# The first adaLN modulation loaded and computed in two halves of 512 features, in a two-layer diffusion trunk

## The chip, the cores and the metric

The kernel runs on one core of a Trainium2 chip. The metric is the device time of one execution in microseconds; the figure given is the median of several executions.

## The reference

The reference is a trunk of two layers over 256 context tokens and 256 latent tokens of width 1024 in float32. Each layer normalises the tokens and modulates them by a conditioning vector (adaLN), projects them by one wide matrix `w_in`, feeds three token mixers (an S5 state-space model, a bidirectional SSD, a windowed attention), merges them, and then runs 16 SwiGLU experts. What the change touches is the modulation at the head of layer 0. Cut to that:

```python
def rmsnorm(x, g):
    xf = x.astype(F32)
    y = xf * lax.rsqrt(jnp.mean(xf * xf, axis=-1, keepdims=True) + EPS)
    return (y * g.astype(F32)).astype(x.dtype)
...
```

The conditioning vectors `c` and `c_ctx` pass through SiLU and are multiplied with `w_mod` (1024 x 6144 for a layer), plus `b_mod`. Of the six vectors of 1024 features that come out, the first two are the shift `sh1` and the scale `sc1` of the first normalisation: the tokens become `rmsnorm(x, norm1_g) * (1 + sc1) + sh1`, with one pair for the context and one for the latent tokens.

## The kernel before, in words

The kernel is written as a sequence of tile operations, and a scheduler orders the instructions of each engine from that sequence. Within an engine the order is then fixed: an instruction that waits holds up all behind it. SP issues the loads, in the order in which the scheduler places them. PSUM banks come from three rings (`mm` 3, `ps` 4, `s5` 1); weight tiles `w` of 0.52 MB come from a ring of three (line 107), with the split into a high and a low part, `wh` on ACT (line 114) and `wl` on DVE or POOL in turn (line 117).

At the head of layer 0, `mixing` (line 464) loads the tokens into `xna` and `xnb` (line 506). `mod_load(k)` (line 490) loads, for a block k of 128 features, the columns of `w_mod` for shift (kind 0) and scale (kind 1): two loads of 0.52 MB each, in runs of 128 floats, 512 B. Blocks 0 to 4 are loaded ahead of the norm, blocks 5 to 7 after the first input projection weights. Blocks 0 and 1 lie in `rb8` tiles, the others in `m8` tiles.

`norm_rows` (line 527) goes over the blocks. For each it calls `mod_unit` (line 148) for both kinds: eight products with `sil` (32 columns of the array each, four column groups, 128 weight columns wide, line 152), a copy of the four partial sums to SBUF on ACT (line 154), a product with `sel2` that sums the groups and turns the result into a column (line 155), and an affine step on ACT that adds the bias and multiplies by the norm weight (line 160). Then `transposed` (line 246) turns the four token tiles of this block (line 249), ACT modulates them into `hrow` (line 252), and DVE splits them into `hh` and `hl` (lines 534 and 535).

The input projection of the S5 part follows in two halves `kh` of four blocks (lines 565 to 577), into four `ps` banks, with three products per weight (`mm3`, lines 126 and 129). Its result goes to DRAM through `us` (lines 561 and 562) and is read back by the S5 loop. That loop also needs the S5 parameters, which `s5_params` computes from 18.7 us on with many small operations on DVE (lines 301 to 309), four copies on ACT (line 421), and a chain on POOL (lines 438 to 443, and 671 to 673). They are independent of the modulation, but are queued on the same engines. `todo` (line 580) holds the other modulations; `mod_group` (line 163) makes them later, between other work. The small projection at line 753 makes the SSD's step sizes.

Of the kernel before, what the change touches and what calls it, by code (L numbers as in the profile page):

```python
# [24 lines left out]
F32 = mybir.dt.float32  # L25
# [3 lines left out]
AF = mybir.ActivationFunctionType  # L29
OP = mybir.AluOpType  # L30
# [41 lines left out]
def tile_trunk(ctx: ExitStack, tc: tile.TileContext, a, out, dbg=None, stop=None):  # L72
# [22 lines left out]
    def K(name):  # L95
        lo, hi = K_OFF[name]
        return kc[:, lo:hi]

    def C(name):
        lo, hi = C_OFF[name]  # L100
        return cl[:, lo:hi]
# [43 lines left out]
    names = ("sh1", "sc1", "g1", "sh2", "sc2", "g2")  # L145
    todo = []

    def mod_unit(l, kind, k, w):
        ps = bank("mm")
        for i in range(8):  # L150
            j = i % 4
            PE.matmul(ps[32 * j:32 * j + 32, :128], sil[:, i, :], w[:, i, :], start=i < 4, stop=i >= 4)
        part = small.tile([128, 128], F32, name="cpart", bufs=2)
        S.activation(part, ps[:, :128], AF.Copy)
        PE.matmul(ps[:, 256:258], part, K("sel2"), start=True, stop=True)
        if k == 0:
            mods[l][names[kind]] = const.tile([128, 8, 2], F32, name="mcol%d_%d" % (l, kind))
        bo = (l * 6 + kind) * 8 + k
        ng = {1: C("norm1"), 4: C("norm2")}.get(kind)
        S.activation(mods[l][names[kind]][:, k, :], ps[:, 256:258], AF.Identity, bias=bmod[:, bo:bo + 1],  # L160
                     scale=1.0 if ng is None else ng[:, l * 8 + k:l * 8 + k + 1])

    def mod_group(l, kind, h):
        ps = bank("mm")
# [303 lines left out]
    def mixing(l, mods):  # L468
# [17 lines left out]
        junk = m8("junk")  # L486
        xv = lambda tt: half(xna[tt // 2], tt)
        if full:
            mw = {}
            slab = Slab(rb, 2)  # L490

            def mod_load(k):
                if k < 2:
                    t = rb.tile([128, 2048], F32, name="rb8", tag="rb8", bufs=NRB)
                else:
                    t = m8("mw").rearrange("p a b -> p (a b)")
                ws = t[:, :1024], t[:, 1024:]
                mw[k] = [w.rearrange("p (i c) -> p i c", i=8) for w in ws]
                for kind in range(2):
                    SP.dma_start(mw[k][kind], a["w_mod"][l][:, kind * D + k * 128:kind * D + k * 128 + 128]  # L500
                                 .rearrange("(i p) c -> p i c", p=128))

            for k in range(0):
                mod_load(k)
            for st, nm in enumerate(("ctx", "x")):
                SP.dma_start(xna[st].rearrange("p (q e) c -> p q (e c)", q=2), a[nm].rearrange("(q p) d -> p q d", p=128))
            for k in range(0, 5):
                mod_load(k)
            xn = norm_tok([0, 1, 2, 3], xv, xv, lambda tt: half(junk, tt))
        else:  # L510
            xo = X["x"]
            xn = {}
            for st in range(2):
                rs = rs_tok(X["xsq"], [2 * st, 2 * st + 1])
                for i in range(2):
                    tt = 2 * st + i
                    xn[tt] = xv(tt)
                    if i:
                        S.activation(xn[tt], xo[:, tt, :], AF.Copy, scale=rs[:, i:i + 1])
                    else:  # L520
                        V.tensor_scalar(xn[tt], xo[:, tt, :], rs[:, i:i + 1], None, op0=OP.mult)
            xsave = dram.tile([256, D], F32, name="xsave")
            SP.dma_start(xsave.rearrange("(q p) d -> p q d", p=128), xo[:, 2:4, :])
            X["stack"].close()
        bst = ExitStack()
        bp = bst.enter_context(tc.tile_pool(name="mixB", bufs=1, side="right", reuse_waits="tile"))
        def norm_rows(ks):
            for k in ks:
                if full:
                    for kind in range(2):  # L530
                        mod_unit(0, kind, k, mw[k][kind])
                h = transposed(xn, [0, 1, 2, 3], k, mods["sc1"], mods["sh1"], bp, "t2", T2,
                               ("mm" if k % 2 else "s5") if full else "ps")
                V.tensor_copy(r(hh[:, k, :]), h)
                (G if k % 2 and not full else V).tensor_tensor(r(hl[:, k, :]), h, hh[:, k, :], op=OP.subtract)
# [28 lines left out]
        if full:  # L564
            ub = [bank() for _ in range(4)]
            for kh in range(2):
                norm_rows(range(4 * kh, 4 * kh + 4))
                wu = []
                for i in range(0, 4, 2):
                    wu.append(load_w(a["w_in"][l], 4 * kh, 4, 128 * i, 256))  # L570
                if kh == 0:
                    for k in range(5, 8):
                        mod_load(k)
                for i in range(0, 4, 2):
                    wh, wl = wu[i // 2]
                    mm3(ub[i:i + 2], wcols(wh, wl), [lambda m, k=k: hv(4 * kh + k, 0, 512) for k in range(4)], kh == 0, kh == 1)
            for m in range(4):
                ev_u(m, ub[m])
        else:
            norm_rows(range(8))  # L580
            win(0, [0] * 4, ev_u)
# [1014 lines left out]
```

## Time and profile before

| | us |
|---|---|
| median of three executions | 2152.39 |
| lowest of three | 2150.96 |
| highest of three | 9962.31 |
| the profiled execution, its own time | 2158.89 |
| its span, first to last instruction | 2157.1 |
| PE (TensorE) busy in the span | 1887.0 |
| DVE (VectorE) busy | 1049.4 |
| ACT (ScalarE) busy | 560.5 |
| POOL (GpSimd) busy | 585.1 |

Busy times are sums over the whole span, over stages with different limits. PEld are TensorE's weight loads, which overlap its products; a float32 product is two instructions in the trace. The granted clock of TensorE was 0.945 of full speed over the span. The profile moved 561.7 MB, 260 GB/s on average.

### The profile page before, as it was taken

Reading aid. Unit: us, or ns where it says so; the run is one execution under the profiler, and the core shown is the slowest. Engines: PE = TensorE matmul, PEld = TensorE weight load, DVE = VectorE, ACT = ScalarE, POOL = GpSimd, SP = SyncE. Lnnn points to the kernel's source line nnn. Section 1 sums busy time; section 2 is a strip of 40 time slices with the busy share of each in tenths; the row PEclk is TensorE's granted clock in tenths of the full one; section 3 lists DMA queues with packets and bytes.
Section 4 is the critical chain, followed back from the end, with each engine's and each line's share of the span. In section 5 each row is a group of like instructions: output and inputs, shape, how many; then the busy total and the mean of one; then the engine's idle time right before and its main releaser. Section 6 shows DMA issues by size and latency. Waiting matters only on the chain.

```text
span 2157.1 us, 29435 instructions
## 1 busy us (share of the span) xinstructions
PE 1887.0 (87%) x11292; PEld 1127.7 (52%) x11292; DVE 1049.4 (49%) x2250; ACT 560.5 (26%) x1216; POOL 585.1 (27%) x644
## 2 busy tenths in 40 slices
PE   6899989999999999787887798989999898777775
PEld 4577767788787333222222576778898432111111
DVE  6888787763246226221212569777856322112112
ACT  4425634442343120000000433534444110000000
POOL 1645476542242000200001425475633100000000
PEclk9899999999999999999999897988999899999998
DMA  9464333336346989799999265342476999999996
GB/s 275 152 189 130 109 90 108 100 104 215 98 147 243 412 324 418 319 420 420 419 420 362 77 200 166 119 125 74 110 248 205 420 420 420 419 420 420 420 420 260
DMA packets 214460, 561.70 MB, mean 260 GB/s; under 512 B 41328, under 2 KB 129840, under 8 KB 165936
## 3 DMA queue, kind: packets, MB, share of 16 engines
q1 hardware_dynamic: 182016, 541.82, 66.8%
q10 hardware_dynamic: 32304, 18.00, 3.0%
q8 instruction: 89, 1.46, 0.3%
q14 instruction: 51, 0.42, 0.1%
HBM read 552.00 MB, written 7.77 MB: 260 GB/s over the span
## 4 chain that ended last, share of the span: by engine, by line
PE 48%; DMA 33%; DVE 11%; POOL 3%; issue 2%; ACT 2%; SPq 1%; DVEq 0%; POOLq 0%; ACTq 0%
PE bk_mm L126 12%; PE bk_mm L129 6%; DMA xw<-w_e_up 6%; DMA xw<-w_e_gate 4%; DMA xw<-w_e_down 4%; DMA xq<-w_e_down 4%; PE bk_mm L1415 4%; DMA rb<-w_e_gate 3%; DMA rb<-w_e_down 3%; DMA xq<-w_e_up 3%; PE bk_ps L1304 3%; DMA w<-w_in 2%; PE bk_mm L1431 2%; PE bk_mm L1445 2%; DMA xq<-w_e_gate 2%
## 5 line engine op out<-in xcount | busy, mean ns | idle before, releaser
L126 PE MATMUL bk_mm<-hh,wh 128*128 128x512 f32 (+1 forms) x704 | 255.0, 375 | 8.3 <-ACT xp L806 4.6
L126 PE MATMUL bk_mm<-hl,wh 128*128 128x512 f32 (+1 forms) x704 | 247.7, 365 | 0.0
L117 POOL TENSOR_TENSOR wl<-w,wh 128x1024 fp32r<-128x1024 f32 x64 | 156.8, 2450 | 221.1 <-ACT wh L114 175.8
L114 ACT ACTIVATE wh<-w 128x1024 fp32r<-128x1024 f32 x140 | 148.1, 1058 | 227.2 <-PE bk_mm L126 107.7
L129 PE MATMUL bk_mm<-hh,wl 128*128 128x512 f32 (+1 forms) x704 | 161.9, 360 | 0.0
L126 PEld LDWEIGHTS bk_mm<-hh,wh 128*128 128x128 f32 x704 | 140.0, 199 | 32.0 <-ACT xp L806 6.0
L126 PEld LDWEIGHTS bk_mm<-hl,wh 128*128 128x128 f32 x704 | 139.8, 199 | 17.4 <-issue 1.0
L117 DVE TENSOR_TENSOR wl<-w,wh 128x1024 fp32r<-128x1024 f32 x76 | 101.6, 1338 | 77.0 <-ACT wh L114 36.3
L129 PEld LDWEIGHTS bk_mm<-hh,wl 128*128 128x128 f32 x704 | 119.1, 195 | 17.6 <-issue 1.2
L1450 DVE SCALAR_TENSOR_TENSOR hd<-fth,bk_mm 64x512 f32<-64x512 f32 x16 | 10.9, 681 | 220.3 <-ACT fth L1448 220.3
L1435 DVE SCALAR_TENSOR_TENSOR YE<-bk_mm,grow 32x512 f32<-32x512 f32 x64 | 43.9, 687 | 133.8 <-PE bk_mm L1431 133.0
L1448 ACT ACTIVATE fth<-bk_mm 64x512 f32<-64x512 f32 x16 | 9.4, 590 | 364.5 <-PE bk_mm L1445 364.5
L1415 PE MATMUL bk_mm<-xw,xeB 128*64 128x512 f32 x368 | 88.0, 601 | 15.6 <-DMA xw<-w_e_up 9.5
L1467 DVE SCALAR_TENSOR_TENSOR YE<-bk_mm,grow 32x512 f32<-32x512 f32 x64 | 44.0, 687 | 104.7 <-PE bk_mm L1462 103.9
L1445 PE MATMUL bk_mm<-xw,xeB 128*32 128x512 f32 x296 | 68.0, 597 | 18.5 <-DMA xw<-w_e_gate 9.8
L609 POOL MEMSET rb<- 128x256 f32 x2 | 1.2, 588 | 286.1 <-DMA rb<-w_e_gate 272.9
L1418 ACT ACTIVATE fth<-bk_mm 128x512 f32<-128x512 f32 x16 | 9.6, 597 | 239.7 <-PE bk_mm L1415 239.7
L169 PE MATMUL bk_mm<-w,sil 128*32 128x128 f32 x1280 | 60.8, 291 | 9.5 <-DMA w<-w_mod 8.5
L1431 PE MATMUL bk_mm<-xw,hT 128*64 128x512 f32 x232 | 62.0, 628 | 7.2 <-ACT hT L1426 5.2
L1392 PE MATMUL bk_ps<-YE,Gt 128*128 128x512 f32 x128 | 61.0, 610 | 6.3 <-DVE YE L1435 3.2
L1415 PEld LDWEIGHTS bk_mm<-xw,xeB 128*64 128x64 f32 x368 | 24.1, 136 | 77.5 <-issue 35.7
L126 PE MATMUL bk_mm<-yh,wh 128*128 128x512 f32 (+1 forms) x192 | 63.9, 349 | 0.8 <-ACT yh L741 0.8
(564 smaller groups left out, 3914.7 us busy)
## 6 DMA issues: line engine op xcount, KB each, us to landing
xw<-w_e_up SPq DMA_DIRECT2D x70, 1024.0 KB, 19.9
xw<-w_e_gate SPq DMA_DIRECT2D x62, 1024.0 KB, 19.9
xw<-w_e_down SPq DMA_DIRECT2D x58, 1024.0 KB, 19.8
w<-w_in SPq DMA_DIRECT2D x92, 512.0 KB, 4.2
w<-w_mod SPq DMA_DIRECT2D x80, 512.0 KB, 3.8
rb<-w_e_down SPq DMA_DIRECT2D x36, 1024.0 KB, 19.9
rb<-w_e_gate SPq DMA_DIRECT2D x35, 1024.0 KB, 14.2
rb<-w_e_up SPq DMA_DIRECT2D x33, 1024.0 KB, 19.9
```

Source lines behind the costliest of these rows:

```text
L114: S.activation(r(hi), raw, AF.Copy)
L117: e.tensor_tensor(r(lo), raw, hi, op=OP.subtract)
L126: PE.matmul(ps, wh(m, k), xv, start=first and k == 0 and i == 0, stop=False)
L129: PE.matmul(ps, wl(m, k), xs[k](m)[0], start=False, stop=last and k == n - 1)
L169: PE.matmul(ps[32 * j:32 * j + 32, :128], sil[:, 2 * u + i, :], w[:, i, pair(j) if kind in (3, 4) else slice(j * 128, j * 128 + 128)], sta ...
L1304: PE.matmul(ps[:, si * w_:si * w_ + w_], x[:, tt, pair(k)], oh[tt][:, e0:e1, :], start=q == 0, stop=q == 1)
L1392: PE.matmul(ps, Gt[:, tt - tts[0], e // ne, :], YE[:, tt // 2 if full else 0, n, :], start=True, stop=True)
L1415: PE.matmul(ps[64 * n:64 * n + 64, :], xeT(k, e), w[:, n * 512:n * 512 + 512], start=k == 0, stop=k == 7)
L1431: PE.matmul(py[64 * n:64 * n + 64, :], hT[:, k // 4, k % 4, :], w, start=k == 0, stop=k == 7)
L1435: V.scalar_tensor_tensor(YE[q0:q0 + 32, si, n, :], py[o:o + 32, :], 0.5, g2[o:o + 32, si, n * 512:n * 512 + 512], op0=OP.mult, op1=OP.mult)
L1445: PE.matmul(pg[o:o + 32, :], xeT(k, e), w[:, n * 512:n * 512 + 512], start=k == 0, stop=k == 7)
L1467: V.scalar_tensor_tensor(YE[q0:q0 + 32, 0, n, :], py[o:o + 32, :], 0.5, g2[o:o + 32, 1, n * 512:n * 512 + 512], op0=OP.mult, op1=OP.mult)
```

## The change

The modulation of the first normalisation is made in two halves h of 512 features. `mod_load(h, u, kind, own)` loads, for a half h and a kind, 512 rows (half u of the contraction) by 512 columns: 1.05 MB in runs of 512 floats, 2 KB. There are eight such loads where there were sixteen; the four of half 0 stand ahead of the norm, the four of half 1 after the first weights of the input projection. `mod_half` uses four column groups of 32 for two kinds times two parities, 512 columns wide, copies the whole bank on ACT, transposes it in four pieces (four products with `ident`), and lets DVE sum the two partial sums (a reduction straight from PSUM), multiply by the norm weight and add the bias. It is called once per half, ahead of `norm_rows`.

```diff
-    def mod_unit(l, kind, k, w):
+    def mod_half(h, ws):
         ps = bank("mm")
...
+        for kind, u, w in ws:
+            for i in range(4):
+                j = 2 * kind + i % 2
+                PE.matmul(ps[32 * j:32 * j + 32, :], sil[:, 4 * u + i, :], w[:, i, :], start=u == 0 and i < 2, stop=u == 1 and i >= 2)
+        part = small.tile([128, 512], F32, name="mpart", bufs=1)
+        S.activation(part, ps, AF.Copy)
+        pt = bank("mm")
+        for j in range(4):
+            PE.transpose(pt[:, j * 128:j * 128 + 128], part[:, j * 128:j * 128 + 128], ident)
+        pv = pt.rearrange("p (j k a s) -> p k j s a", j=4, k=2, a=2)
+        for kind in (1, 0):
+            if h == 0:
+                mods[0][names[kind]] = const.tile([128, 8, 2], F32, name="mcol0_%d" % kind)
+            dst = mods[0][names[kind]][:, 4 * h:4 * h + 4, :]
+            bc = lambda v: v[:, :, None].to_broadcast([128, 4, 2])
+            V.tensor_reduce(dst, pv[:, kind, :, 0:2, :], axis=AX.X, op=OP.add)
+            if kind:
+                V.tensor_tensor(dst, dst, bc(C("norm1")[:, 4 * h:4 * h + 4]), op=OP.mult)
+            bo = kind * 8 + 4 * h
+            V.tensor_tensor(dst, dst, bc(bmod[:, bo:bo + 4]), op=OP.add)
...
+            def mod_load(h, u, kind, own):
+                w = (rb.tile([128, 2048], F32, name="rb8", tag="rb8", bufs=NRB) if own
+                     else m8("mw").rearrange("p a b -> p (a b)")).rearrange("p (i c) -> p i c", i=4)
+                c0 = kind * D + h * 512
+                SP.dma_start(w, a["w_mod"][l][512 * u:512 * u + 512, c0:c0 + 512].rearrange("(i p) c -> p i c", p=128))
+                mw.setdefault(h, []).append((kind, u, w))
...
-            for k in range(0, 5):
-                mod_load(k)
+            for u in range(2):
+                for kind in range(2):
+                    mod_load(0, u, kind, u == 0)
...
             for k in ks:
-                if full:
-                    for kind in range(2):
-                        mod_unit(0, kind, k, mw[k][kind])
...
             for kh in range(2):
+                mod_half(kh, mw[kh])
                 norm_rows(range(4 * kh, 4 * kh + 4))
...
                 if kh == 0:
-                    for k in range(5, 8):
-                        mod_load(k)
+                    for u in range(2):
+                        for kind in range(2):
+                            mod_load(1, u, kind, False)
```

The scheduler orders all engines anew. The first place is DVE shortly after the norm. Line numbers of the changed kernel are those of its own text: its 309, 311, 314, 317 and 339 are lines 301, 303, 306, 309 and 331 before (S5 parameters), its 260 is 252, its 429 is 421, and 534 and 535 are the same; `rb` is the S5 parameters' scratch, `hh` and `hl` the split tokens, `mcol` the modulation columns. Before:

```order
L306 SCALAR_TENSOR_TENSOR rb_112<-rb_112 128x96 x6
L534 CAST hh<-hrow 128x512
L309 TENSOR_TENSOR rb_112<-rb_112 128x96 x2
L535 TENSOR_TENSOR hl<-hrow,hh 128x512
L303 TENSOR_SCALAR rb_112<-rb_112 128x96
L534 CAST hh<-hrow 128x512
L303 TENSOR_SCALAR rb_112<-rb_112 128x96
L535 TENSOR_TENSOR hl<-hrow,hh 128x512
L301 TENSOR_SCALAR rb_112<-rb_112 128x96 x2
L306 SCALAR_TENSOR_TENSOR rb_112<-rb_112 128x96 x2
```

After:

```order
L309 TENSOR_SCALAR rb_112<-rb_112 128x96 x2
L314 SCALAR_TENSOR_TENSOR rb_112<-rb_112 128x96
L165 TENSOR_REDUCE mcol_1_182<-bk_mm 128x8
L165 TENSOR_REDUCE mcol_0_186<-bk_mm 128x8
L314 SCALAR_TENSOR_TENSOR rb_112<-rb_112 128x96
L167 TENSOR_TENSOR mcol_1_182<-mcol_1_182,cl 128x8
L169 TENSOR_TENSOR mcol_0_186<-mcol_0_186,cl 128x8
L309 TENSOR_SCALAR rb_112<-rb_112 128x96
L311 TENSOR_SCALAR rb_112<-rb_112 128x96
L169 TENSOR_TENSOR mcol_1_182<-mcol_1_182,cl 128x8
L314 SCALAR_TENSOR_TENSOR rb_112<-rb_112 128x96
L339 CAST rb_112<-rb_112 128x96
```

Before, the S5 operations there were interleaved with the first splits `hh` and `hl`, one block after the other; now the two reductions and the three further steps of the first half stand there, and the first split comes later, behind more S5 operations.

The second place is DVE in the second half, where `hh` of block 5 was made. Before:

```order
L309 TENSOR_TENSOR rb_113<-rb_112 128x64 x2
L309 TENSOR_TENSOR rb_112<-rb_113 128x64 x4
L534 CAST hh<-hrow 128x512
L309 TENSOR_TENSOR rb_113<-rb_112 128x64 x2
L535 TENSOR_TENSOR hl<-hrow,hh 128x512
L309 TENSOR_TENSOR rb_112<-rb_112 128x64 x2
```

After:

```order
L317 TENSOR_TENSOR rb_112<-rb_113 128x64 x4
L317 TENSOR_TENSOR rb_113<-rb_112 128x64 x2
L165 TENSOR_REDUCE mcol_1_182<-bk_mm 128x8
L165 TENSOR_REDUCE mcol_0_186<-bk_mm 128x8
L317 TENSOR_TENSOR rb_112<-rb_112 128x64 x2
L317 TENSOR_TENSOR rb_112<-rb_112 128x32
L167 TENSOR_TENSOR mcol_1_182<-mcol_1_182,cl 128x8
L169 TENSOR_TENSOR mcol_0_186<-mcol_0_186,cl 128x8
```

The reduction of the second half has come to the place where a split of block 5 stood, behind the same S5 operations.

The third place is ACT, from the last modulations of the second half to the last `hrow`; `sp_aa` and `sp_ab` are the copies of the S5 parameters. Before:

```order
L160 ACTIVATE mcol_1_191<-bk_mm,cl 128x2
L252 ACTIVATE hrow<-bk_mm,mcol_0_177,mcol_1_191 128x256 x2
L154 ACTIVATE cpart<-bk_mm 128x128 x2
L421 ACTIVATE sp_aa<-rb_113 64x8x4x9
L421 ACTIVATE sp_ab<-rb_113 64x8x4x9
L160 ACTIVATE mcol_0_177<-bk_mm,cl 128x2
L154 ACTIVATE cpart<-bk_mm 128x128
L421 ACTIVATE sp_aa<-rb_113 64x8x4x9
L421 ACTIVATE sp_ab<-rb_113 64x8x4x9
L160 ACTIVATE mcol_1_191<-bk_mm,cl 128x2
L252 ACTIVATE hrow<-bk_s_478,mcol_0_177,mcol_1_191 128x256 x2
```

After:

```order
L114 ACTIVATE wh<-w 128x1024 x2
L155 ACTIVATE mpart<-bk_mm 128x512
L429 ACTIVATE sp_aa<-rb_113 64x8x4x9
L429 ACTIVATE sp_ab<-rb_113 64x8x4x9
L429 ACTIVATE sp_aa<-rb_113 64x8x4x9
L429 ACTIVATE sp_ab<-rb_113 64x8x4x9
L260 ACTIVATE hrow<-bk_s_326,mcol_0_186,mcol_1_182 128x256 x2
L260 ACTIVATE hrow<-bk_mm,mcol_0_186,mcol_1_182 128x256 x2
L260 ACTIVATE hrow<-bk_s_346,mcol_0_186,mcol_1_182 128x256 x2
```

Before, two of the four `hrow` pairs of the second half stood ahead of the S5 copies (the earlier one is not in this piece) and two behind them (the later one is not in it); now all four stand behind the four copies, the last one outside the piece.

## Rows read from the trace of the kernel before

**Rows 1.** Windows by stage: length, busy (count) of PE, PEld, DVE, ACT, POOL, clock, DMA, GB/s.

```profile
46.00:54.00 8.00, 7.01 (x105) 5.73 (x96) 7.97 (x48) 3.96 (x10) 0.61 (x1) 1.00 0.51 139
...
100.00:310.00 210.00, 195.82 (x1576) 149.13 (x1572) 173.32 (x316) 102.88 (x254) 113.58 (x128) 0.97 0.45 133
...
400.00:620.00 220.00, 220.00 (x1193) 174.55 (x1182) 100.98 (x180) 80.11 (x143) 85.94 (x76) 1.00 0.43 130
...
880.00:1185.00 305.00, 256.73 (x1053) 77.85 (x1050) 58.34 (x88) 13.50 (x26) 6.36 (x10) 0.99 1.00 412
1185.00:1690.00 505.00, 452.31 (x3414) 377.81 (x3416) 354.43 (x710) 204.56 (x446) 240.22 (x247) 0.89 0.50 157
```

**Rows 2.** Chain of waits, 0 to 33 us: start, length, what.

```profile
11.10 1.69 SPq L500
...
23.71 1.74 SPq L110
...
25.49 7.79 DMA w<-w_in
```

**Rows 3.** Timeline of PE, 13 to 46 us: start, length, what, idle before.

```profile
13.16 1.08 PE L152 MATMUL bk_mm<-rb,sil 128*32 128x128 f32 x16 [13.16 <-DMA rb<-w_mod]
...
24.22 1.08 PE L152 MATMUL bk_mm<-mw,sil 128*32 128x128 f32 x32
25.80 0.64 PE L152 MATMUL bk_mm<-mw,sil 128*32 128x128 f32 x16 [0.50 <-DMA mw<-w_mod]
...
32.91 0.80 PE L126 MATMUL bk_ps<-hh,wh 128*128 128x512 f32 x1 [1.48 <-ACT wh L114]
...
43.79 1.98 PE L129 MATMUL bk_ps<-hh,wl 128*128 128x512 f32 x8
```

**Rows 4.** Timeline of DVE, 18 to 53 us, columns as in rows 3.

```profile
18.69 0.20 DVE L303 TENSOR_SCALAR rb<-rb 128x96 f32<-128x96 f32 x1
...
23.61 0.43 DVE L534 CAST hh<-hrow 128x512 fp32r<-128x512 f32 x1 [1.06 <-ACT hrow L252]
...
34.39 2.00 DVE L117 TENSOR_TENSOR wl<-w,wh 128x1024 fp32r<-128x1024 f32 x1 [1.70 <-ACT wh L114]
...
52.78 0.42 DVE L534 CAST hh<-hrow 128x512 fp32r<-128x512 f32 x1
```

**Rows 5.** Waits of DVE, 18.69 to 62.2 us: for whom, total, times, longest.

```profile
DVE hh L534 <- ACT hrow L252: 2.9, 5, 1.1
```

**Rows 6.** Timeline of POOL, the chain after DVE, columns as in rows 3.

```profile
62.25 0.27 POOL L438 TENSOR_TENSOR rb<-sp_e8r,rb 128x32 f32<-128x32 f32 x1 [4.59 <-DVE rb L309]
...
81.17 0.72 POOL L673 TENSOR_TENSOR rb<-rb 128x256 f32<-128x256 f32 x1
```

**Rows 7.** Windows by DMA load, columns as in rows 1.

```profile
3.00:11.00 8.00, 0.00 (x0) 0.00 (x0) 1.42 (x13) 3.23 (x9) 0.00 (x0) 1.00 1.01 386
...
18.00:22.00 4.00, 4.00 (x42) 2.83 (x41) 3.69 (x16) 1.05 (x4) 0.53 (x1) 1.00 1.16 290
...
83.00:86.00 3.00, 1.99 (x8) 1.89 (x9) 2.93 (x10) 2.84 (x8) 1.99 (x3) 0.62 1.07 368
```

**Rows 8.** Timeline of PE, the projection with four column groups.

```profile
58.58 1.06 PE L753 MATMUL bk_mm<-hh,w 128*32 128x512 f32 x8
```

**Rows 9.** Timeline of ACT, 53 to 71 us, columns as in rows 3.

```profile
53.36 0.74 ACT L421 ACTIVATE sp_aa<-rb 64x288 f32<-64x288 f32 x1 [1.59 <-DVE rb L309]
...
57.03 1.02 ACT L252 ACTIVATE hrow<-bk_s,mcol,mcol 128x256 f32<-128x256 f32 x2
...
70.72 0.60 ACT L561 ACTIVATE us<-bk_ps 128x512 f32<-128x512 f32 x1 [0.40 <-PE bk_ps L129]
```

**Rows 10.** Timeline of DVE, a small operation with a PSUM source.

```profile
83.87 0.16 DVE L186 TENSOR_TENSOR mcol<-bk_mm,cl 128x8 f32<-128x8 f32 x1
```

**Rows 11.** Lines of ACT, 0 to 72 us: group, count, busy, mean ns, idle before.

```profile
L160 ACT ACTIVATE mcol<-bk_mm,cl 128x2 f32<-128x2 f32 x16 | 4.8, 308 | 6.9 <-PE bk_mm L155 6.9
L154 ACT ACTIVATE cpart<-bk_mm 128x128 f32<-128x128 f32 x16 | 4.2, 273 | 6.9 <-PE bk_mm L152 6.8
```

More of the change, by code (lines that the diff above doesn't have):

```diff
@@ L146, in tile_trunk @@
     todo = []
-    def mod_unit(l, kind, k, w):
+    def mod_half(h, ws):
         ps = bank("mm")
[L150 to L161, printed above, removed]
+        for kind, u, w in ws:
[18 more added lines that the diff above has]
+            V.tensor_tensor(dst, dst, bc(bmod[:, bo:bo + 4]), op=OP.add)
     def mod_group(l, kind, h):
@@ L488, in mixing @@
         if full:
+            slab = Slab(rb, 2)
             mw = {}
[L490 to L498, printed above, removed]
-                for kind in range(2):
-                    SP.dma_start(mw[k][kind], a["w_mod"][l][:, kind * D + k * 128:kind * D + k * 128 + 128]
-                                 .rearrange("(i p) c -> p i c", p=128))
-            for k in range(0):
-                mod_load(k)
+            def mod_load(h, u, kind, own):
[4 more added lines that the diff above has]
+                mw.setdefault(h, []).append((kind, u, w))
             for st, nm in enumerate(("ctx", "x")):
                 SP.dma_start(xna[st].rearrange("p (q e) c -> p q (e c)", q=2), a[nm].rearrange("(q p) d -> p q d", p=128))
-            for k in range(0, 5):
-                mod_load(k)
+            for u in range(2):
+                for kind in range(2):
+                    mod_load(0, u, kind, u == 0)
             xn = norm_tok([0, 1, 2, 3], xv, xv, lambda tt: half(junk, tt))
@@ L528, in norm_rows @@
             for k in ks:
-                if full:
-                    for kind in range(2):
-                        mod_unit(0, kind, k, mw[k][kind])
                 h = transposed(xn, [0, 1, 2, 3], k, mods["sc1"], mods["sh1"], bp, "t2", T2,
@@ L571, in mixing @@
                 if kh == 0:
-                    for k in range(5, 8):
-                        mod_load(k)
+                    for u in range(2):
+                        for kind in range(2):
+                            mod_load(1, u, kind, False)
                 for i in range(0, 4, 2):
```

## The prediction

> **What bounds the kernel now.** I read the windows by stage first, then the chain of waits at the start, then the timelines of the engines that this chain meets. The end of the kernel is set by the weight stream of the experts: from 880 to 1185 us the transfers run at 412 GB/s with a share of 1.00 [rows 1]. In front of it stands the first mixing layer, and its later part is TensorE alone: from 400 to 620 us PE is busy 220.00 of 220 us [rows 1]. So a microsecond won or lost at the start reaches the end only if TensorE's work between 70 and 400 us moves with it.
>
> The change lies in the first 70 us. There the chain of waits is at first the queue of loads: each half-megabyte load of the modulation weights holds SP for 1.69 us, the first load of the input projection is issued at 23.71 and lands 7.79 us after the issue ended [rows 2]. TensorE gets its first modulation weights at 13.16, waits again at 25.80 for the eighth load, and starts the input projection at 32.91 [rows 3]. After that the bound changes. DVE works off the S5 parameters (the small operations at lines 301 to 309) from 18.69 on [rows 4], and from 46 to 54 us it is busy 7.97 of 8 us [rows 1]. Its last result releases POOL at 62.25, and POOL's chain ends with the row at 81.17 (0.72 long), 81.9 us [rows 6]. That chain opens the S5 loop. Between 18.69 and 62.2 DVE waited 2.9 us for ACT's hrow, in five waits [rows 5], and 1.70 us for wh ahead of 34.39 [rows 4]: 4.6 us of idleness in all. This is all that DVE can win.
>
> **The loads.** Removed are 16 loads of 0.52 MB in 512 B runs, added 8 of 1.05 MB in 2 KB runs. The total stays 8.4 MB, but the first half now needs 4.19 MB ahead of the input projection's weights where 5.24 MB stood. Before, eight loads landed from 13.16 to 25.80, (25.80 - 13.16) / 7 = 1.8 us each, which is the 290 GB/s of 18 to 22 us [rows 3, 7]. No stretch has 2 KB runs alone. The 4 KB runs of the token tiles went at 386 GB/s, a stretch of mixed 1 and 2 KB runs at 368 [rows 7]. The new loads start to flow at 13.16 - 1.8 = 11.4. At 386 they need 10.9 us and are there at 22.2, at 368 11.4 us and 22.8, at 290 14.5 us and 25.8. I take 22.2, since two of the three rows lie close to it, and keep 25.8 for the range.
>
> A rule speaks against this. The Trainium skill, "DMA: Bandwidth & Descriptors", section "Specifications", puts the smallest transfer for line rate at 512 B, so that longer runs would bring nothing; the sum by it is the third rival's. The trace does not agree so far: the 512 B loads stay at 290 GB/s with the engines' share above 1 [rows 7].
>
> **First half on the engines.** TensorE removes 256 instructions of 128 columns (128 matmuls, each two instructions; 32 in 1.08 us [rows 3], 8.6 us) and adds 64 of 512 columns with the same column count. The projection at line 753 has this form with four column groups, 8 in 1.06 us [rows 8]: 64 / 8 x 1.06 = 8.5 us. That is even. The small products with sel2 go, eight transposes come; I count them at nothing, since TensorE waits here anyway. ACT loses 16 copies and 16 affine steps, 4.2 + 4.8 us [rows 11], and gets two copies of 128x512; the nearest row is the 0.60 us eviction at 70.72 [rows 9]. DVE gets ten small operations. TENSOR_REDUCE does not occur in the rows; between 0.16 us (128x8 from PSUM [rows 10]) and 0.43 us (128x512 [rows 4]) I take 0.16, because it also writes 128x8: 1.6 us, at most 4.3.
>
> So, after 22.2: the last load's eight instructions 1.06, copy 0.6, four transposes about 0.6 (an estimate from the 1.08 us for 32 instructions of that width, each now waiting on its own weights) give 24.5. By then DVE, which meets this reduction in its order, has been waiting: it had nothing to do from 23.61 - 1.06 = 22.55 [rows 4], and seven more S5 operations now stand before the reduction, at 0.13 us each (an estimate from the 0.20 of one such row, overlapped) 0.9 us. So it is there near 23.5, and about 1.0 us is new idleness. Five operations with five S5 ones between them take 1.6 (26.1), hrow 1.02 [rows 9] (27.1), hh 0.43 [rows 4] (27.6). The input projection starts there, 5.3 us sooner than 32.91 [rows 3].
>
> **Second half.** The first block of the projection took from 32.91 to 45.8 [rows 3], 12.9 us, so it would end at 40.5. Then come the last 12 products (24 instructions, 3.2 us), copy 0.6 and transposes 0.6: 44.9. But their reduction is queued on DVE behind the S5 parameters, at the place of the hh that began at 52.78 [rows 4]. DVE comes there at 52.78 - 4.6 (idleness gone) - 1.1 (one pair hh/hl fewer ahead of it) + 0.8 (five new operations) + 1.0 (new idleness) = 48.9. On ACT the four S5 copies, which started at 53.36 with 0.74 each [rows 9], now all stand ahead of hrow for k=4: 48.9 + 3.0 + 1.02 = 52.9, with hh 53.4. Before, eight products of the second block ran early and its rest, with other work, from about 53.3 to 70.5, that is 17.2 us. Less the modulation pieces in it (about 3) and plus the eight (about 2) it is 16.2: 69.6 against 70.5, or 70 with the slow first products that 32.91 shows (0.80 for the first [rows 3]). So of TensorE's 5.3 us only 0.5 to 1 is left at the end of this block; TensorE stands from about 44.9 to 53.4 but for some transposes and the small dt projection.
>
> **The sum.** DVE lets POOL go at 62.25 - 4.6 + 1.6 + 1.0 + 0.5 (part of the gaps remains) = 60.75, so 1.5 us sooner; POOL's 20 us are as before. TensorE's block ends 0.5 to 1 us sooner. I take 1.5 us for the whole. The profiled execution took 2158.9 us (span 2157.1 and 1.8 around it); less 1.5 it is 2157.4. It lies 6.5 above the median of the runs, 2152.4, so the forecast for the median is 2151. That is within 2% (43 us), about what a measurement of this kernel can tell from no change.
>
> **Rivals.** *TensorE's gain is kept.* If DVE reaches the second reduction by 45, the block ends 5.3 us sooner and, as TensorE is full later, the kernel does too: 2147. The full windows from 400 us on speak for it, the 7.97 of 8 us on DVE against it [rows 1].
>
> *Second half late, slower.* The place is the reduction behind the S5 parameters. If DVE wins none of its idleness back, it is there at 52.78 + 0.8 or later, hrow starts after ACT's S5 copies at 56.6, hh is there at 58.0, and the block ends at 58.0 + 16.2 + 1 = 75.2, 4.7 us later than before: 2157. It decides from about 50 us on for that reduction. For it speaks that two engines have S5 work ahead of one wait; against it that ACT has 7.8 us less to do [rows 11].
>
> *The longer runs bring nothing.* At 290 GB/s the first half is there at 25.8, DVE waits 1.0 + 3.6 = 4.6 us there, and POOL goes at 62.25 - 4.6 + 1.6 + 4.6 + 0.5 = 64.3, 2.1 us later: 2154.5. The 4 KB row speaks against it [rows 7].
>
> *The rest is dealt anew.* The scheduler writes another order for both mixing layers, though nothing in them changed. TensorE stands 14.2 us from 100 to 310 and 52.7 us from 1185 to 1690 [rows 1]; a quarter of that either way is 15 us, 2136 or 2166. Nothing in the rows says which way.
>
> **How the numbers follow.** Forecast 0.45, TensorE's gain kept 0.2, second half late 0.15, runs bring nothing 0.05, dealt anew by over 8 us 0.15 in equal parts. The likeliest is 2151. The first four cases lie between 2147 and 2157; the last one widens this to 2136 to 2166. All cases stay within 2% but for an unforeseen tail: faster 0.02, same 0.96, slower 0.02.
>
> **What would show it.** Right, if the windows of the loads show well over 290 GB/s, the first product of the projection starts near 27.6, TensorE then idles in the mid-forties until a reduction on DVE near 49, and POOL's chain starts near 60.8. Wrong, if that reduction comes before 46 or after 51, if POOL starts later than 62.25, or if the two spans differ by more than 8 us and the difference arises after 100 us.

## The result, and the profile after

The kernel took 2175.30 us with the change (median of four executions, 2172.88 to 2181.26) and 2151.68 without it: 23.6 us more, a ratio of 1.0103 with an interval from 1.0084 to 1.0123. The ratios in this document compare fast executions of both kernels, and are not the quotients of the medians beside them. The forecast was 2151.0, its range ended at 2166. The profiled execution took 2181.26 us and its span was 2179.5, against 2157.1 before: 22.4 more.

The times at which some things start in the two traces say where this arises:

| | before, us | after, us | difference |
|---|---|---|---|
| POOL's chain after DVE | 62.25 | 62.27 | 0.0 |
| the last `us` eviction | 70.72 | 72.61 | 1.9 |
| fourth S5 row written to `ad` | 300.6 | 297.6 | -3.0 |
| fifth S5 row | 357.0 | 369.3 | 12.3 |
| eighth, last S5 row | 487.1 | 507.3 | 20.2 |
| first GLU product (`aT`, line 1122, now 1124) | 540.0 | 569.6 | 29.6 |
| x of layer 0 saved | 1200.1 | 1229.8 | 29.7 |

The head, which is all that the change edits, ends 1.9 us later. The loss comes in layer 0's mixing, between 300 and 570 us. Behind the save of x the profiled execution of the kernel before took 957.0 us and that of the change 949.7, so that the spans differ by 22.4 and not by 29.7; this is no gain of the change, since the order of the kernel before took 946.2 us there in a run below. The windows by stage, in the columns of [rows 1], with one for the new loads that answers to [rows 7]:

```profile
14.00:18.00 4.00, 2.60 (x8) 0.64 (x8) 2.72 (x14) 0.83 (x2) 0.00 (x0) 1.00 1.04 386
...
46.00:54.00 8.00, 6.96 (x54) 2.71 (x52) 8.00 (x42) 2.63 (x4) 2.19 (x4) 1.00 0.46 132
100.00:310.00 210.00, 190.42 (x1531) 144.56 (x1532) 174.96 (x313) 97.81 (x244) 108.67 (x123) 0.93 0.42 129
400.00:620.00 220.00, 212.89 (x1176) 166.02 (x1176) 98.74 (x198) 76.03 (x145) 77.38 (x77) 0.96 0.41 122
880.00:1185.00 305.00, 252.10 (x1062) 77.93 (x1064) 74.71 (x189) 14.71 (x24) 18.35 (x45) 0.98 0.97 401
1185.00:1690.00 505.00, 454.16 (x3432) 370.07 (x3428) 343.64 (x686) 205.29 (x447) 241.78 (x250) 0.92 0.50 158
```

TensorE, which had no idle time from 400 to 620 us [rows 1], now has 7.1 us there, and 5.4 us more from 100 to 310. Its clock is lower in both. (The last two windows do not hold the same work as before, which has moved by 30 us.) One window from 70 us to the first GLU product, the same work in both kernels, gives the account; before:

```profile
70.00:540.00 470.00, 449.86 (x3264) 350.34 (x3263) 337.63 (x677) 202.46 (x479) 246.46 (x274) 0.97 0.45 137
```

and after:

```profile
70.00:569.60 499.60, 465.87 (x3266) 360.72 (x3266) 339.54 (x677) 203.57 (x481) 248.54 (x273) 0.94 0.42 128
```

The instruction counts agree within three. Idle time rose from 470.00 - 449.86 = 20.1 to 499.60 - 465.87 = 33.7 us, 13.6 more; busy time rose by 16.0 for the same products, at a mean granted clock of 0.94 instead of 0.97. These make the 29.6 us.

Two places carry most of the waits. The first is TensorE's wait for the convolution on DVE. PE's waits from 100 to 310 us, before (engine, line, for whom: total, times, longest):

```profile
PE bk_mm L126 <- ACT xp L806: 3.5, 2, 3.3
PE bk_ps L928 <- ACT qm L926: 2.0, 2, 1.4
```

and after:

```profile
PE bk_mm L126 <- ACT xp L808: 5.1, 2, 3.6
PE bk_ps L852 <- DVE BC L824: 5.1, 1, 5.1
PE bk_ps L858 <- DVE xw L849: 2.3, 1, 2.3
```

The wait for `BC` is new. It is followed by TensorE at a lower clock; windows of 160 to 210 us, before and after:

```profile
160.00:210.00 50.00, 45.69 (x375) 35.30 (x376) 45.12 (x83) 28.32 (x77) 27.79 (x30) 0.98 0.41 125
```

```profile
160.00:210.00 50.00, 46.11 (x348) 36.11 (x348) 40.29 (x80) 24.05 (x63) 20.70 (x26) 0.83 0.43 134
```

The seventh convolution result (the line's operation `BC`) left DVE at 156.96 us before and at 167.78 after; the timeline of DVE, before and after:

```profile
156.96 0.69 DVE L822 SCALAR_TENSOR_TENSOR BC<-cth,yh 128x512 f32<-128x512 f32 x1
```

```profile
167.78 0.68 DVE L824 SCALAR_TENSOR_TENSOR BC<-cth,yh 128x512 f32<-128x512 f32 x1
```

DVE was not slower: it was busy 52.6 of 60 us from 100 to 160 before and 57.3 after. Its order gave the time to S5 work, whose first row came out 10.5 us sooner (151.9 against 162.4 us).

The second place is behind the last S5 row. Before, only the attention's last four transposes were left then; TensorE had gates and branch products (lines 126 and 129) and no wait. Before, from 487.1 us to the first GLU product:

```profile
L126 PE MATMUL bk_mm<-yh,wh 128*128 128x512 f32 x28 | 10.7, 389 | 0.0
L129 PE MATMUL bk_mm<-yh,wl 128*128 128x512 f32 x32 | 8.4, 389 | 0.0
L1056 PE MATMUL bk_ps<-kc,yt 128*128 128x128 f32 x4 | 0.6, 271 | 0.0
```

After, the groups of PE from 507.3 us to the first GLU product show attention still going on (`pT`, line 1045), waits for `yh` and `wl`, and branch products of 444 to 465 ns each where they took 389 before:

```profile
L126 PE MATMUL bk_mm<-yh,wh 128*128 128x512 f32 x26 | 11.3, 444 | 1.3 <-ACT yh L743 1.3
...
L129 PE MATMUL bk_mm<-yh,wl 128*128 128x512 f32 x32 | 10.5, 465 | 2.8 <-DVE wl L117 2.8
L1045 PE MATMUL bk_ps<-vt,pT 128*128 128x64 f32 x16 | 2.0, 275 | 0.0
L1058 PE MATMUL bk_ps<-kc,yt 128*128 128x128 f32 x4 | 0.6, 279 | 1.2 <-DVE yt L1055 1.2
```

### The profile page after: what moved, and what is told of

Read it like the earlier page. It is cut to its first block, busy times and chain, and to the rows that moved or that the text cites. A ratio compares the mean times of both kernels' runs of the same rounds, so it can differ in the third digit from the quotient of the medians.

```text
span 2179.5 us, 28948 instructions
## 1 busy us (share of the span) xinstructions
PE 1892.5 (87%) x11076; PEld 1121.5 (51%) x11076; DVE 1048.7 (48%) x2260; ACT 553.7 (25%) x1186; POOL 588.6 (27%) x644
## 4 chain that ended last, share of the span: by engine, by line
PE 35%; DMA 30%; DVE 8%; ACT 1%; issue 1%; POOL 1%; DVEq 0%; SPq 0%; ACTq 0%; POOLq 0%
PE bk_mm L126 8%; DMA xw<-w_e_up 5%; DMA xw<-w_e_gate 5%; PE bk_mm L1417 4%; PE bk_mm L129 4%; DMA xq<-w_e_down 4%; DMA xw<-w_e_down 4%; DMA rb<-w_e_up 3%; DMA rb<-w_e_gate 3%; DMA rb<-w_e_down 3%; PE bk_mm L1433 2%; PE bk_ps L1306 2%; PE bk_mm L1447 2%; DMA xq<-w_e_gate 2%; PE bk_ps L1394 1%
## 5 line engine op out<-in xcount | busy, mean ns | idle before, releaser
L126 PE MATMUL bk_mm<-yh,wh 128*128 128x512 f32 (+1 forms) x192 | 68.3, 372 | 1.3 <-ACT yh L743 1.3
L126 PE MATMUL bk_mm<-yl,wh 128*128 128x512 f32 (+1 forms) x192 | 66.8, 364 | 0.5 <-POOL yl L1130 0.3
L1447 PE MATMUL bk_mm<-xw,xeA 128*32 128x512 f32 x272 | 60.4, 610 | 5.1 <-DMA xw<-w_e_up 4.7
```

The source lines that it names most:

```text
L126: PE.matmul(ps, wh(m, k), xv, start=first and k == 0 and i == 0, stop=False)
L1447: PE.matmul(pg[o:o + 32, :], xeT(k, e), w[:, n * 512:n * 512 + 512], start=k == 0, stop=k == 7)
```

## The experiments

The theory after the comparison: the new head is worth about nothing, and the loss is the order that the scheduler gives to all that follows, though none of it was edited. The rivals: the head itself costs (1.9 us later, and what grows from it), or only part of the rest matters.

**The order exchanged.** All instructions traced behind layer 0's S5 parameters, 11,866 of them, are the same in both kernels. The first run takes the changed kernel and gives each engine the order that these instructions had in the kernel before; the second takes the kernel before with the order from the changed one. The order is held by dependencies that carry no semaphore (shortened: the packing of the tables is left out, and `NOSYNC` stands for such a dependency):

```diff
+    for row in ORDER:
+        prev = None
+        for pos in row:
+            if prev is not None:
+                tc.add_manual_dep(tail[pos], prev.name, NOSYNC, reason="order")
+            prev = tail[pos]
```

> The changed kernel, with every instruction that is traced behind the S5 parameters of layer 0 (11,866 of them, both layers) issued on each engine in the order that the kernel before has. Only the head is new. Theory 'order' (the 23 us come from the order in which the rest was dealt anew, the head itself costs 1 to 2 us): 2152 to 2156. Theory 'head' (the late second half of the modulation delays what follows, whatever the order): 2170 to 2176.

> The kernel before, with the same 11,866 instructions issued in the order of the changed kernel. Only the order of the rest is new. Theory 'order': 2170 to 2176. Theory 'head': 2150 to 2156.

New head with old order: 2150.39 us, ratio 0.9975 [0.9959, 0.9990]. Old head with new order: 2178.03, ratio 1.0102 [1.0076, 1.0128], as slow as the whole change; the kernel before took 2155.64 on that chip. Both times lie 2 us outside the range of theory 'order' and some 20 us from that of theory 'head'. In the first the GLU product is back at 540.4 us, and the account of TensorE is that of the kernel before:

```profile
70.00:540.40 470.40, 449.87 (x3262) 350.89 (x3262) 339.60 (x671) 202.25 (x479) 246.05 (x271) 0.97 0.45 137
```

In the second it starts at 570.6, and TensorE's wait for `BC` is there again, without a line of the change in the kernel:

```profile
PE bk_ps L861 <- DVE BC L833: 5.1, 1, 5.1
```

**Any new order.** Is it this order, or every order that the scheduler finds? Both kernels got an edit that moves no work, only the two loads of a pair (here in the kernel before, likewise in the changed one):

```diff
-                for kind in range(2):
+                for kind in (1, 0):
```

> The kernel before, with one edit that changes no work: of each block the scale's weights are loaded ahead of the shift's. The scheduler deals the rest anew (2,788 of TensorE's 7,373 later places hold another instruction). Theory 'order': the time moves by 5 to 25 us either way, although the head does not change. Theory 'head': 2150 to 2154.

> The changed kernel with the same edit (scale's weights loaded ahead of the shift's in each half); the rest is dealt anew once more. Theory 'order': anywhere from 2145 to 2180, and not necessarily near 2175. Theory 'head': 2173 to 2177.

2179.98 us, 1.0101 [1.0081, 1.0120], and 2186.18, 1.0128 [1.0107, 1.0149]. A kernel that does the work of the kernel before lost as much as the change; the second lies 6 us above the range that was expected. The GLU products start at 567.3 and 567.6, with different heads (`us` evictions from 74.1 and from 70.3 us, where they start at 67.6 in the kernel before). So the swap moves the head too, which its expectation took to be unchanged; only the exchange of orders separates head and rest.

**Which part of the order.** Four runs hold a part of the old order in the changed kernel and leave the rest to the scheduler: all of layer 0's mixing; what is traced up to the end of its SSD passes; what is traced behind them, to the end of layer 0's mixing; and, for the loads' run length (further down), all of it with loads cut in four. The second holds those instructions whose names stand in `X["ys"]`, the list of what is traced up to there:

```diff
+            if tail[pos].name in X["ys"]:
```

> The changed kernel, with the old order kept on every engine for what the program traces from the S5 parameters to the end of layer 0's mixing; the expert layers and layer 1 are ordered anew. Theory (the loss is the new order of layer 0's mixing alone): the first GLU product starts at 538 to 545 us as in the kernel before (540.0; 569.6 with the change), TensorE's idle time from 70 us to that product is 20 us and not 34, the granted clock there 0.97, and the kernel takes 2145 to 2160 us. Rival (the new order of later stages costs as well): first GLU product at 540 but a time of 2163 us or more, with the difference behind 1185 us. Rival (the modulation itself costs): first GLU product at 550 or later and 2165 or more.

> The changed kernel with the old order kept only for what is traced up to the end of layer 0's two SSD passes, with the first four S5 blocks; attention, gates, branch products and all behind them are ordered anew. Theory A (the loss is made in the SSD part, by 300 us): S5 rows as before (fourth at 299 to 303 us, last at 485 to 490), first GLU product at 538 to 546, time 2145 to 2160. Theory B (the loss is made where the attention is dealt among gates and branch products): fourth S5 row still at 299 to 303, but the last at 500 or later, first GLU product at 560 to 572, TensorE idle 6 us or more in the 75 us around the end of the S5 loop, and 2168 to 2182.

> The reverse: the changed kernel, free order up to the end of layer 0's SSD passes, old order kept from there to the end of layer 0's mixing, free behind it. Theory A (loss made in the SSD part): last S5 row at 495 or later, first GLU product at 550 to 570, 2160 to 2180. Theory B (loss made in the attention part): last S5 row at 485 to 495, first GLU product at 538 to 550, TensorE without idle time in the 75 us around the end of the S5 loop, 2145 to 2163.

| old order held in | us | ratio | last S5 row | first GLU product |
|---|---|---|---|---|
| layer 0's mixing | 2166.83 | 1.0035 [0.9999, 1.0072] | 493.7 | 545.6 |
| to the end of the SSD passes | 2164.83 | 1.0063 [1.0045, 1.0081] | 488.5 | 544.4 |
| behind them, in layer 0's mixing | 2172.44 | 1.0104 [1.0033, 1.0174] | 506.6 | 558.4 |

Of the 29.6 us at the GLU product the order up to the SSD's end gives back 25.2, the order behind it 11.2; the two overlap. So the SSD part looks the larger place (theory A of these runs), by one trace each. With the second, the 75 us around the end of the S5 loop have 2.9 us of idle time left, with the third 0.1:

```profile
475.00:550.00 75.00, 72.11 (x337) 57.34 (x337) 30.60 (x51) 21.04 (x32) 20.06 (x18) 0.98 0.56 178
```

```profile
475.00:550.00 75.00, 74.91 (x462) 60.43 (x461) 33.65 (x67) 24.06 (x45) 21.91 (x21) 1.00 0.63 200
```

The first two runs missed their numbers: the GLU product was back, the time was not. Two further runs look for the rest of the loss: layer 0's mixing ordered anew and the old order behind it, and the first run again.

> The complement: the changed kernel with layer 0's mixing ordered anew, as the change has it, and the old order kept behind it (expert layers and layer 1). Theory (the loss is all in layer 0's mixing): first GLU product at 565 to 573 us, and 2170 to 2182, as slow as the change itself. Rival (the later stages' new order costs some 10 us, which the run with layer 0's mixing in the old order, 2166.8, speaks for): first GLU product at 565 to 573, from the save of x to the end 944 to 948 us instead of 949.7, and 2160 to 2168.

> Layer 0's mixing in the old order, all behind it ordered anew, timed again with the complement beside it (it was 2166.8, ratio 1.0035 [0.9999, 1.0072]). If the later stages' new order costs nothing: 2148 to 2157 and a ratio whose interval holds 1. If it costs: 2160 to 2170 and a ratio of 1.003 to 1.007, and the ratios of this run and of the complement add up to about that of the change, 1.010.

The change's order of layer 0's mixing alone: 2174.67 us, 1.0081 [1.0053, 1.0109], GLU product at 563.3. By itself it has most of the loss, and its interval overlaps with that of the whole change, 1.0084 to 1.0123. From the save of x to the end this run took 952.2 us, not the 944 to 948 that the rival wanted; the kernel with the whole old order took 946.2.

The first run again: 2164.21, 1.0042 [1.0019, 1.0065], GLU product at 536.8. This is a loss behind layer 0's mixing, but not the change's own. With layer 0's mixing held, the scheduler gave the rest a third order: compared one by one in the traces, some 1,170 of the 5,114 products behind the save of x stand elsewhere than in the change, and some 940 elsewhere than in the kernel before. So the two ratios are not parts of one sum, though they add up to about that of the change. Of the change's own order the traces show no cost behind layer 0's mixing: from the first GLU product to the end, the change took 1609.9 us and the old head with the change's order 1613.7, while six traces with the old order there (the kernel before, the complement, and the new head with the whole old order in four runs) took 1605.0 to 1617.1. The third order took 1619.4 and 1624.2. The other runs that hold a part of layer 0's mixing have later stages of their own, too; for them the GLU product says more than the time.

**Which engine's order.** Two runs hold one engine alone, up to the end of the SSD passes.

> The changed kernel with VectorE's old order alone, up to the end of layer 0's SSD passes; the other engines and all that follows are ordered anew. Theory (in the new order VectorE has S5 work ahead of the convolutions, and TensorE waits for them): the seventh and eighth convolution results (BC) come at 155 to 159 and 169 to 173 us as before (157.0 and 170.6; 167.8 and 174.7 with the change), TensorE has no wait of 5 us for BC, the first GLU product starts at 540 to 552, and the time is 2150 to 2170. Rival (TensorE's own order loses the time): BC as before, but the first GLU product at 558 or later and 2170 or more.

> The changed kernel with TensorE's old order alone, up to the end of layer 0's SSD passes. Theory (VectorE's order loses the time): the seventh BC later than 162 us, first GLU product at 555 or later, 2168 or more. Rival (TensorE's order decides, and the other engines follow it): seventh BC at 155 to 160, first GLU product at 540 to 552, 2150 to 2168.

With VectorE's old order: 2166.50 us, 1.0057 [1.0034, 1.0081], GLU product at 548.7, no wait of 5 us for `BC`, which is back in place:

```profile
158.76 0.69 DVE L831 SCALAR_TENSOR_TENSOR BC<-cth,yh 128x512 f32<-128x512 f32 x1
```

That is as good as all engines held over this stretch (2164.83). With TensorE's old order `BC` came back too, to 157.9 us, as the rival had it, but the time was 2180.90 (two executions, 1.0128 [1.0082, 1.0174]), as the theory had it; the GLU product at 554.1 lies between the two forecasts. By the times the order of VectorE is the better handle; the GLU products, 5.4 us apart in one trace each, do not decide it. Since each engine follows the one that is held, the two can't be parted by these runs.

**The head by itself.** With the whole old order behind it the head can be measured without the re-dealing. The loads were cut into pieces with 512 B runs:

```diff
-                SP.dma_start(w, a["w_mod"][l][512 * u:512 * u + 512, c0:c0 + 512].rearrange("(i p) c -> p i c", p=128))
+                for b in range(0, 512, 128):
+                    SP.dma_start(w[:, :, b:b + 128], a["w_mod"][l][512 * u:512 * u + 512, c0 + b:c0 + b + 128].rearrange("(i p) c -> p i c", p=128))
```

> The changed kernel with the whole old order kept behind the S5 parameters (its time so was 2150.4), and every modulation load cut into four pieces of 128 columns, which brings the 512 B runs back. If the run length sets the rate: 280 to 300 GB/s from 14 to 22 us instead of 379 to 391, the last first-half products start 3 to 4 us later than with 2 KB runs, the first product of the input projection at 33 to 35 us instead of 30.5, and 2150 to 2156. If longer runs bring nothing: the same 380 GB/s and the first product at 30 to 31 us, 2147 to 2153.

From 14 to 18 us the cut loads, and then the 2 KB runs of the kernel with the old order:

```profile
14.00:18.00 4.00, 3.11 (x8) 0.65 (x8) 3.90 (x21) 0.00 (x0) 0.00 (x0) 1.00 1.21 290
```

```profile
14.00:18.00 4.00, 3.44 (x8) 0.64 (x8) 3.58 (x15) 0.00 (x0) 0.00 (x0) 1.00 1.05 389
```

The run length sets the rate, 290 against 389 GB/s; the kernel before had 512 B runs, half as many loads, and the same 290 [rows 7]. The first product of the projection starts at 35.59 instead of 30.54, POOL's chain at 65.06 instead of 61.50, and the time is 2159.31, 1.0017 [0.9993, 1.0041]; both lie above what was expected. The head was then timed again, and with four column groups for every load (a bank for each kind).

```diff
...
-                j = 2 * kind + i % 2
-                PE.matmul(ps[32 * j:32 * j + 32, :], sil[:, 4 * u + i, :], w[:, i, :], start=u == 0 and i < 2, stop=u == 1 and i >= 2)
...
+                    PE.matmul(ps[32 * i:32 * i + 32, :], sil[:, 4 * u + i, :], w[:, i, :], start=u == 0, stop=u == 1)
```

> The changed kernel with the whole old order behind the S5 parameters, timed again (it was 2150.4, ratio 0.9975 [0.9959, 0.9990]). If the new head is worth the 1.5 us of the forecast or more: a ratio of 0.9965 to 0.9995, the interval below 1. If it is worth nothing: an interval that holds 1. First GLU product at 540 to 541 in both cases.

> As the run before it, but each kind of modulation has a bank of its own, so that every load's four products go to four column groups instead of two; two copies and four transposes more per half. If two column groups made the products slow: 8 instructions in 1.0 to 1.2 us at the full clock instead of 1.91, the first product of the projection 0.5 to 1.5 us before 30.5, POOL's chain at 60.5 to 61.5, and 2145 to 2152, which can't be told from 2150. If the number of groups changes nothing: 8 still in 1.8 to 2.0 us, and the added copies and transposes make the first product 0.5 to 1 us later than 30.5.

Again: 2153.43 us, 0.9989 [0.9968, 1.0009], an interval that holds 1. Four groups: 2153.81, 1.0001 [0.9983, 1.0020]. Eight instructions took 1.06 us with four groups, 1.91 with two; but at the start they took 1.94, and the projection began at 34.16, 3.0 us later than in the run before it (31.18), not sooner. PE with four groups:

```profile
13.94 1.94 PE L162 MATMUL bk_mm<-rb,sil 128*32 128x512 f32 x8 [13.94 <-DMA rb<-w_mod]
...
34.16 1.20 PE L135 MATMUL bk_ps<-hh,wh 128*128 128x512 f32 x4
...
39.42 1.06 PE L162 MATMUL bk_mm<-mw,sil 128*32 128x512 f32 x8
```

and with two:

```profile
18.71 1.91 PE L162 MATMUL bk_mm<-rb,sil 128*32 128x512 f32 x8
...
23.27 1.91 PE L162 MATMUL bk_mm<-mw,sil 128*32 128x512 f32 x8 [0.34 <-DMA mw<-w_mod]
...
31.18 0.80 PE L135 MATMUL bk_ps<-hh,wh 128*128 128x512 f32 x2
```

One thing in these two traces bears on the forecast's sum. POOL's chain, by which it goes, started at 55.51 with four groups, outside the 60.5 to 61.5 expected, and at 62.14 with two:

```profile
55.51 0.31 POOL L454 TENSOR_TENSOR rb<-sp_e8r,rb 128x32 f32<-128x32 f32 x1 [3.08 <-DVE rb L325]
```

```profile
62.14 0.27 POOL L455 TENSOR_TENSOR rb<-sp_e8r,rb 128x32 f32<-128x32 f32 x1 [6.93 <-DVE rb L326]
```

The chain's last row came 5.1 us sooner (75.58 against 80.68), the first S5 row 1.8 us (159.69 against 161.46), and the time was the same.

No version beat the kernel before beyond doubt; the new head with the old order is level with it or some 0.1 to 0.25% faster.

## Why the prediction was wrong

**The step that failed is the term for the order of the rest.** The sum of the forecast has none; it stood only as the last rival, "the rest is dealt anew", which named the mechanism and gave it 0.15, "in equal parts", and "a quarter of that either way is 15 us". Measured, the new order of the rest cost 2178.03 - 2155.64 = 22.4 us with the old head, 1.0102, which is the whole result. Three things were off.

- The chance. The prediction said that the scheduler writes another order for both mixing layers, and still treated a loss by it as rare and a gain as just as likely. All three orders that were dealt anew over the whole rest (the change's, with either head, and those of the two swaps of loads) were slower, by 1.01 to 1.28%. Three orders show that a loss was not rare, and no more; why each is worse than the order of the kernel before, no run shows.
- The size. A quarter of TensorE's idle time stood for the stake (of 14.2 + 52.7 us it is 16.7, not 15, and would still have ended the range at 2169). Measured, the idle time up to the GLU product rose by 13.6 us. That this is close is luck, since 7.1 of it came in a stretch that had no idle time, and the 52.7 us from 1185 to 1690 did not rise; and the busy time of the same products rose by 16.0 beside it, at a lower granted clock, for which the term had nothing.
- The place. "From 400 to 620 us PE is busy 220.00 of 220 us" was read as proof that TensorE sets the pace there. It was full because the order had gates and branch products left to lay beside the attention. With another order the same stretch has 7.1 us of idle time.

**The head, step by step.** Its sum, 1.5 us gained, came out in sign and rough size: 0.9975 and 0.9989 in two sets of runs with the old order, some 5 and 2 us, the second with an interval that holds 1. That is luck. POOL's chain, which was to bring the 1.5 us, started at 61.50 and 62.14 in these runs, 0.75 and 0.1 us sooner than 62.25, and the run with four groups shows that 5 us won in that chain need not reach the end. Its terms were less good. PE's rows in the head:

```profile
15.40 3.63 PE L153 MATMUL bk_mm<-rb,sil 128*32 128x512 f32 x8 [15.40 <-DMA rb<-w_mod]
...
19.37 2.28 PE L153 MATMUL bk_mm<-rb,sil 128*32 128x512 f32 x8
...
22.06 3.32 PE L153 MATMUL bk_mm<-mw,sil 128*32 128x512 f32 x16
26.08 0.66 PE L158 MATMUL bk_mm<-kc,mpart 128*128 128x128 f32 x4 [0.70 <-ACT mpart L155]
...
31.68 1.20 PE L126 MATMUL bk_ps<-hh,wh 128*128 128x512 f32 x2
```

- *The loads* came at 381 to 391 GB/s, as taken (386). The rival "the longer runs bring nothing" is refuted by the cut loads at 290. The Trainium skill, "DMA: Bandwidth & Descriptors", section "Specifications", puts line rate from 512 B on; the trace of the cut loads does not agree. The last load was there at 23.27 (a run with the old order, where TensorE waits for it), 1.1 us behind the forecast's 22.2.
- *TensorE's price.* "64 / 8 x 1.06 = 8.5 us" took a projection with four column groups. Each new load feeds only two (`j = 2 * kind + i % 2`), and measured were 3.63 + 2.28 + 3.32 us for the first half and 1.91 + 3.63 for the second, 14.8 us. The last products of the first half ended at 25.4, not 23.3. Beside the groups, the start is slow: [rows 3] had shown 16 instructions in 1.08 us at 13.16 and 32 in the same time at 24.22, and the prediction took the second price for all.
- *DVE's small operations.* 0.16 us was right for the reductions (0.26 for two), and wrong for one product:

```profile
26.77 0.26 DVE L165 TENSOR_REDUCE mcol<-bk_mm 128x8 f32<-128x16 f32 x2 [0.96 <-PE bk_mm L158]
26.95 0.25 DVE L314 SCALAR_TENSOR_TENSOR rb<-rb 128x96 f32<-128x96 f32 x1
27.11 2.31 DVE L167 TENSOR_TENSOR mcol<-mcol,cl 128x8 f32<-128x8 f32 x1
29.34 0.15 DVE L169 TENSOR_TENSOR mcol<-mcol,cl 128x8 f32<-128x8 f32 x1
```

  It stood while POOL's split of a weight ran beside it, from 27.06 to 29.40 (the section on the hardware has the rows). So the projection began at 31.68, not 27.6: 1.2 us before [rows 3], not 5.3.
- *The second half.* The reduction was at 51.98, forecast 48.9, and POOL's chain at 62.27, forecast 60.75:

```profile
51.98 0.24 DVE L165 TENSOR_REDUCE mcol<-bk_mm 128x8 f32<-128x16 f32 x2
```

  What failed here is DVE's work and not its waits. From 18.69 to 62.2 us DVE's waits fell from 4.6 to 1.0 us, as the sum had it; its busy time rose from 38.1 to 41.7, 3.6 us where the sum had 1.6, and 2.2 of this are the one product above. The prediction's own conditions ("after 51", "later than 62.25") were met: the rival "second half late, slower" describes the head better than the forecast did, with 1.9 us at the block's end where it had 4.7. Its 2157 was not the reason for the result, since the same head with the old order took 2150 to 2153.
- *DVE as the bound there*, 8.00 of 8 us from 46 to 54, was right.

The test written at the end held: the spans differ by more than 8 us and the difference arises after 100 us. The change also stayed within 2%, to which the prediction gave 0.96.

## What to carry to other kernels

Where a scheduler orders a whole program, an edit is two changes: the work it edits, and a new order for everything behind it. Look at how far the order moves before forecasting, and give the second its own term, from the waits that the present order avoids and the clock that falls with them; measure the first with the old order held. A stretch in which an engine is always busy is a property of the order too, and can be lost by an edit that never touches it.

## What the hardware showed that was not expected

**A small VectorE operation can stand for 2 us beside POOL.** At this place in the head, in five traces, a small DVE instruction just after the start of POOL's 128x1024 split (`wl`) takes about as long as that split has left to run: a 128x8 product 2.31 us (three times; the addition of the same form behind it takes 0.15), a 128x96 operation of line 314 2.11 us where it takes 0.25, a 128x96 conversion 2.82 where it takes 0.20. POOL in the changed kernel:

```profile
27.06 2.34 POOL L117 TENSOR_TENSOR wl<-w,wh 128x1024 fp32r<-128x1024 f32 x1 [4.79 <-ACT wh L114]
```

27.06 + 2.34 = 29.40, and 27.11 + 2.31 = 29.42 on DVE. It is not so for every instruction: with the cut loads, where the split ran from 30.62, the two reductions from PSUM at 30.80 took their 0.26 and the next instruction, with both its ends in SBUF, 2.11; later in the changed kernel a 128x512 operation with a source in PSUM took 0.69 at 289.50 beside a split, as usual. The Trainium skill, "Trainium Architecture — The Big Picture", section "What this means for kernel authors", says that DVE and GpSimd share a pair of ports under an exclusive lock; the slow rows agree with it. No run here separated the lock from another cause.

**The same eight products took 1.94 us at 13.9 us and 1.06 at 39.4, with a granted clock of 1.00 in the windows of both.** This is the kernel with four groups. With two groups it was 3.63 at the start and 1.91 later; TensorE had been idle up to the first. The granted clock does not tell these apart. In the run with four groups, in which TensorE paused between the loads, they still took 1.93 at 24.67; with two, where it was busy from 15.2 to 22.9, they had come to 1.91 by 18.7. What faster products could have won there went elsewhere anyway: with four groups the last transposes were done at 28.5 us, and DVE came to their reduction at 31.26, behind S5 operations.

**An identical order scatters.** The changed head with the whole old order had its first GLU product at 540.4 in one profile and 546.1 in another; the kernel with layer 0's mixing held, at 545.6 and 536.8. Each pair was taken on two chips, so executions and chips are not told apart. A single profile places a loss of 20 us, and not one of 5.
